# An odd mixer's running sums spread by DMA instead of by matmul, its heads worked in pairs, and each pair's products queued later

## The chip, the cores and the metric

The kernel runs on one core of a Trainium2 chip. The metric is the device time of one execution in microseconds, as the median of several runs. The engines are PE (TensorE, the matmuls), ACT (ScalarE), DVE (VectorE), POOL (GpSimd) and SP (SyncE, which issues most DMAs). Each takes its own queue of instructions in order and waits for others by semaphores.

## What is computed

One inference step of a two-layer decoder trunk: 256 prompt tokens and 8 sequences of 4 sampled tokens (288 columns in all), model width 2048, f32 data. Layer 0 mixes tokens by a gated MLP and sparse attention, layer 1 (the odd one) by a Mamba-2 scan, and each layer ends in a gated feed-forward block. The change touches the scan of layer 1 alone: 64 heads in 8 groups, 128-token chunks for the prompt, 4-token chunks for the samples.

```python
def segsum(a):
    t = a.shape[-1]
    cs = jnp.cumsum(a, axis=-1)
    d = cs[..., :, None] - cs[..., None, :]
    return jnp.where(jnp.tril(jnp.ones((t, t), bool)), d, NEG)

def ssd(x, dt, a, bm, cm, h0):
...
    da = (dt * a).reshape(b, c, q, g, e).transpose(0, 3, 4, 1, 2)
    acs = jnp.cumsum(da, axis=-1)
    cb = jnp.einsum('bcign,bcjgn->bgcij', cc, bc)
    mix = cb[:, :, None] * jnp.exp(segsum(da))
    y_diag = jnp.einsum('bgecij,bcjgep->bcigep', mix, xdt)
...
    y_off = jnp.einsum('bcign,bcgepn->bcigep', cc, st[:, :-1]) * jnp.exp(acs).transpose(0, 3, 4, 1, 2)[..., None]
```

For each head the running sums `acs` have to stand along the free axis in every partition (index i), so that those of index j, one to a partition, can be taken from them.

## The kernel before

The projections set the pace. Every weight matrix is streamed from HBM in loads of 512 KB (`load_w`, line 636; five buffers `wraw`, 8 blocks of 128x128 each), and `convert` (line 644) cuts each half of a load, called a piece here, into a high part `whi` (ACT) and a low part `wlo` (DVE), four pieces ahead of PE. A block then costs three products of 128x288 (high by high, high by low, low by high), so a piece is 12 matmuls.

The program is written out by a planner when it is built. `Clock` holds a model of the engines' times, each instruction is an `Op`, and jobs (generators) hand their instructions to `step` (line 561). A job may yield an instruction, a number (it sleeps for so many planned us), a list of tiles (it sleeps until the planner believes them ready), or a wish for a buffer. An instruction goes into its engine's queue at the point of the main loop at which the planner believes that it can start; for PE, 0.4 us (`HOP` and `MARGIN`) are added behind another engine. A DMA is planned with 2.0 us and its bytes at 360 GB/s (lines 395 and 397). Jobs made with `back` take turns, three at a time, and leave at most 2.5 us of work planned ahead on an engine. The real engines wait by semaphores, so a wrong plan costs waits, not errors.

Phase m1 is the odd mixer. Its projection yields, for each of 8 groups, B, C, four x blocks (`xbc`, through a convolution) and four gates (`z`). With the fourth gate of a group the scan's job `ssd(g)` (line 1213) starts; the fourth gate's evacuation first waits for the norm of the group before (`evac_z`, line 1195, `finish_ssd`). `ssd` transposes x and B, forms the masked products `cbm`, the end state `st`, and starts in the background `ssd_old` (the old states' part, into `xdd`), four `ssd_heads` (one for each pair of heads, line 1324) and `ssd_norm` (line 1379). `ssd_new` updates and stores eight states meanwhile: a product `xst` by `bst` into PSUM, a scaling of `h0` on POOL, an addition on DVE (h<-h,ps), a store by SP.

In `ssd_heads` each head is worked by itself: PE multiplies a column of a selector matrix (`selc`, 128 rows) by the running sums, held as high and low halves in `csh`, which gives the sums in all 128 partitions of a PSUM bank (`pl`); ACT takes Relu of three parts with each partition's own sum as bias into `L`, an exponential of the second chunk into `ec`, and two exponentials of `L`; POOL multiplies `ec` by C; DVE multiplies `L` by `cbm` into `mx` (prompt) and `mxs` (samples). There are two buffers of `L`, four each of `mx`, `ec` and `mxs`. After the second head a `Burst` of 20 products of the pair (`mx`, `ec`, `srep`, `mxs`) goes into PE's queue, and its result passes through DVE and POOL into y and the sum of squares. All PSUM tiles named `ps` come from five banks. All instructions have the planner's line, L391, in the profile; so tiles' names tell them apart.

Of the kernel before, what the change touches and what calls it, by code (L numbers as in the profile page):

```python
# [18 lines left out]
PT, ST, T = 256, 32, 288  # L19
# [103 lines left out]


MATS = {}
for _n, _w in (("tle", 128), ("tgt", 128), ("ble", 32), ("bgt", 32), ("selc", 64), ("srep", 32), ("srepT", 128),
               ("tmask", 256)):
    MATS[_n] = (sum(w for _, w in MATS.values()), _w)
NMAT = sum(w for _, w in MATS.values())
# [2 lines left out]
def const_mats():  # L132

    i = np.arange(128)
    t = np.arange(ST)
    same = t[:, None] // NS == t // NS
    m = dict(
        tle=i[:, None] <= i, tgt=i[:, None] > i,
        ble=same & (t[:, None] <= t), bgt=same & (t[:, None] > t),
        selc=i[:, None] % 64 == np.arange(64),  # L140
        srep=i[:, None] % 32 == t, srepT=t[:, None] == i % 32,
        tmask=np.broadcast_to(np.arange(NB)[:, None] == t // NS, (128, NB, ST)).reshape(128, -1),
    )
    out = np.zeros((128, NMAT), np.float32)
    for k, v in m.items():
        out[:v.shape[0], MATS[k][0]:MATS[k][0] + v.shape[1]] = v
    return out
# [374 lines left out]
class Trunk:  # L522
# [137 lines left out]
    def run(self):  # L660
        tc, nc = self.tc, self.nc
        with ExitStack() as st:
            pool = lambda n, b, **k: Slots(st.enter_context(tc.tile_pool(name=n, bufs=b, **k)), b, self.clk)
            self.cst = pool("cst", 1)
            self.wraw = pool("wraw", 5)
            self.wsp = pool("wsp", AHEAD + 1)
            self.xp = pool("xp", 1)
            self.rms = pool("rms", 4)
            self.hsp = pool("hsp", 1, space=bass.MemoryType.DRAM).tile([128, KD, T], F32, name="hsp")
            self.pmain = pool("pmain", PMAIN, space=bass.MemoryType.PSUM)  # L670
            self.pold = pool("pold", 1, space=bass.MemoryType.PSUM)
            self.pside = pool("pside", 7 - PMAIN, space=bass.MemoryType.PSUM)
            st.enter_context(tc.manual_schedule())
            self.body()
# [343 lines left out]
    def enter_m1(self, l):  # L1018
        nc = self.nc
        self.job(self.make_rstd())  # L1020
        self.nbg = 3
        one = self.pool("one", 1)
        self.wk = self.pool("wk", 2)
        self.w3 = self.pool("w3", 3)
        self.w4 = self.pool("w4", 4)
        self.w8 = self.pool("w8", NB)
        self.zr = self.pool("zr", 12)
        t = lambda name, shape, dt=F32: one.tile(shape, dt, name=name)
        self.cmat = t("cmat", [128, NMAT])
        nc.sync.dma_start(self.cmat, self.I["cmat"])  # L1030
        self.y2 = t("y2", [128, 16, T])
        self.cx = deque(t(f"cx{i}", [128, 315]) for i in range(3))
        for c in self.cx:
            nc.gpsimd.memset(c[:, 0:3], 0.0)
        self.sw = t("sw", [128, 48, 5])
        self.selc = t("selc", [128, 64], F32R)
        self.dtt = t("dtt", [128, 3, 64])
        self.dat = t("dat", [128, 3, 64])
        self.cs = t("cs", [128, 3, 64])
        self.dec = t("dec", [128, 3, 64])  # L1040
        self.ecr = t("ecr", [128, 64])
        self.et1 = t("et1", [128, 64])
        self.ets = t("ets", [128, NB, 64])
        self.csh = t("csh", [128, T], F32R)
        self.xdt = t("xdt", [128, 2, 512])
        self.xdd = t("xdd", [128, 2, 512])

        self.xds = t("xds", [128, 512])
        nc.gpsimd.memset(self.xds[64:128], 0.0)
        self.mxs = deque(t(f"mxs{i}", [128, ST]) for i in range(4))  # L1050
        for z in self.mxs:
            nc.gpsimd.memset(z, 0.0)
        self.xst = t("xst", [96, 512], F32R)
# [12 lines left out]
        self.job(self.odd_consts())  # L1066
        self.job(self.load_h(), 20.0)

    def odd_consts(self):
        nc = self.off  # L1070
        yield nc.vector.tensor_scalar(self.sw[:, :, 0:4], self.P("sw", 0, 192).rearrange("p (c k) -> p c k", k=4), 0.5, None,
                                      op0=OP.mult)
        yield nc.vector.tensor_scalar(self.sw[:, :, 4], self.P("sb", 0, 48), 0.5, None, op0=OP.mult)
        yield nc.vector.tensor_copy(self.selc, self.M("selc"))
        self.flags.add("consts")

    def load_scv(self, g):
# [15 lines left out]
    def dt_chain(self, z):  # L1093
        nc, wk = self.off, self.w3
        e = yield wk.want([64, T], F32, name="dz")
        q = yield wk.want([64, T], F32, name="dz")
# [18 lines left out]
        ps = yield self.pside.want([128, 2, 3, 64], F32, name="ps")  # L1115
# [22 lines left out]
        yield self.mm(p2[:, 0:128], da[:, 0], self.M("tle"), start=True, stop=True)  # L1138
        yield self.mm(p2[:, 128:256], da[:, 1], self.M("tle"), start=True, stop=True)
        yield self.mm(p2[:, 256:288], das, self.M("ble", 32), start=True, stop=True)  # L1140
        yield nc.scalar.copy(self.csh[:64], p2)
        yield nc.vector.tensor_tensor(self.csh[64:128], p2, self.csh[:64].bitcast(F32), op=OP.subtract)
        self.rel(p2)
        p3 = yield self.pside.want([128, 512], F32, name="ps")
        yield self.mm(p3, self.ones[:32].to_broadcast([32, 128]), dam.rearrange("p b h -> p (b h)"), start=True, stop=True)
        yield nc.scalar.activation(self.ets.rearrange("p b h -> p (b h)"), p3, AF.Exp)
# [177 lines left out]
    def ssd_heads(self, g, q):  # L1324

        nc, wk = self.off, self.wk
        C = self.C[g]
        mx, ce, ms = [], [], []
        for e in range(2):
            h = 8 * g + 2 * q + e  # L1330
            m = yield self.w4.want([128, PT], F32, name="mx")
            ec = yield self.w4.want([128, 128], F32, name="ec")
            L = yield wk.want([128, T], F32, name="L")
            pl = yield self.pside.want([128, T], F32, name="ps")
            yield self.mm(pl, self.selc[:, h:h + 1].to_broadcast([128, 128]), self.csh, start=True, stop=True)
            for lo, hi, r, c in ((0, 128, 128, 0), (128, 256, 128, 1), (256, 288, 32, 2)):
                yield nc.scalar.activation(L[:r, lo:hi], pl[:r, lo:hi], AF.Relu, bias=self.cs[:r, c, h:h + 1], scale=-1.0)
            yield nc.scalar.activation(ec, pl[:, 128:256], AF.Exp)
            self.rel(pl)
            yield nc.scalar.activation(L[:, :PT], L[:, :PT], AF.Exp, scale=-1.0)  # L1340
            yield nc.scalar.activation(L[:32, PT:], L[:32, PT:], AF.Exp, scale=-1.0)
            yield nc.gpsimd.tensor_tensor(ec, ec, C[:, 128:256], op=OP.mult)
            yield nc.vector.tensor_tensor(m[:, :PT], L[:, :PT], self.cbm[:, :PT], op=OP.mult)
            while not self.mxs:
                yield 0.3
            z = self.mxs.popleft()
            yield nc.vector.tensor_tensor(z[:32], L[:32, PT:], self.cbm[:32, PT:], op=OP.mult)
            ms.append(z)
            self.rel(L)
            mx.append(m)  # L1350
            ce.append(ec)
        while "old" not in self.sdone:
            yield 0.4
        py = yield self.pside.want([128, T], F32, name="ps")

        oh = [(e, py[64 * e:64 * e + 64], slice(128 * q + 64 * e, 128 * q + 64 * e + 64)) for e in range(2)]
        ops = [self.mm(o[:, 0:128], self.xdt[:, 0, hc], mx[e][:, 0:128], start=True, stop=True) for e, o, hc in oh]
        ops += [self.mm(o[:, 128:256], self.xdt[:, 1, hc], mx[e][:, 128:256], start=True, stop=False) for e, o, hc in oh]
        ops += [self.mm(o[:, 128:256], self.st[:, hc], ce[e], start=False, stop=True) for e, o, hc in oh]
        ops += [self.mm(o[:, 256:288], self.xdd[:, 0, hc], self.M("srep"), start=True, stop=False) for e, o, hc in oh]  # L1360
        ops += [self.mm(o[:, 256:288], self.xds[:, hc], ms[e], start=False, stop=True) for e, o, hc in oh]
        yield Burst(ops)
        self.mxs.extend(ms)
        k = 4 * g + q
        y = self.yraw(k)
        yield nc.vector.scalar_tensor_tensor(y, y, self.P("sd", k), py, op0=OP.mult, op1=OP.add)
# [904 lines left out]
```

## Time and profile before

| | us |
|---|---|
| median of 3 runs | 3082.39 |
| lowest and highest run | 3081.61, 3086.01 |
| profiled execution, its time | 3080.35 |
| profiled execution, its span | 3078.6 |

The profile is of one execution. Busy time of an engine is the time in which it worked on an instruction. PE's rows give a matmul's own duration; they overlap in the pipeline, so a busy PE may take a new product every 133 ns while each lasts 295. PEld, the weight load, is a row of its own. "Idle before" is the time an engine stood still just ahead of an instruction, and the name behind it is what ended the wait.

### The profile page before, as it was taken

What the parts mean: (1) busy time and instruction counts of PE and PEld (TensorE: products, weight loads), DVE (VectorE), ACT (ScalarE), POOL (GpSimd) and SP (SyncE); (2) the same over time, 40 slices, a digit from 0 to 9 for tenths busy, and PEclk for the clock granted to TensorE, in tenths of its full rate; (3) what the DMA queues carried; (4) which work ended last, traced back from release to release, by engine and by line L of the source; (5) the groups of instructions that cost most, each with busy time, mean ns of one, the idle gap of its engine ahead of it and who ended that gap; (6) DMA issues with size and microseconds to landing.
All of it is one profiled execution on the core that took longest, in us unless ns stands there. A gap on an engine that the chain in (4) does not pass through costs nothing.

```text
span 3078.6 us, 62211 instructions
## 1 busy us (share of the span) xinstructions
PE 3043.6 (99%) x23073; PEld 2943.9 (96%) x23073; DVE 2166.0 (70%) x4593; ACT 1614.4 (52%) x3229; POOL 724.6 (24%) x1029
## 2 busy tenths in 40 slices
PE   9999999999999999999999999999999999999999
PEld 8887889999999999999999999999999999999999
DVE  7876567775577557668888888885777647755764
ACT  6766545554455445555555555554455435544553
POOL 4535433100000000123445555530310000000000
PEclk8999999999999999999999999999999999999999
DMA  8987885444444444564555555554454444444454
GB/s 316 348 282 249 277 282 176 165 165 165 164 165 165 165 166 164 184 222 142 188 198 191 191 191 185 196 179 174 161 172 166 166 166 164 165 165 165 165 177 146
DMA packets 189760, 587.41 MB, mean 191 GB/s; under 512 B 23280, under 2 KB 43280, under 8 KB 189456
## 3 DMA queue, kind: packets, MB, share of 16 engines
q1 hardware_dynamic: 170256, 516.31, 48.7%
q0 software_dynamic: 19200, 67.12, 6.3%
q8 instruction: 182, 2.98, 0.4%
q14 instruction: 122, 1.00, 0.1%
HBM read 555.57 MB, written 27.78 MB: 189 GB/s over the span
## 4 chain that ended last, share of the span: by engine, by line
PE 89%; DVE 4%; POOL 3%; issue 1%; DMA 1%; ACT 1%; SPq 0%; DVEq 0%; ACTq 0%; POOLq 0%
PE acc L391 79%; PE ps L391 9%; DVE wlo L391 1%; PE po L391 1%; POOL ec L391 1%; DVE h L391 1%; DMA st<-in_ccmp,ptc 1%; POOL ssq L391 1%; POOL nrm L391 1%; DVE cv L391 1%; ACT whi L391 0%; DMA st<-in_cselv,ptv 0%; DVE mxs L391 0%; POOL st L391 0%; ACT L L391 0%
## 5 line engine op out<-in xcount | busy, mean ns | idle before, releaser
L391 DVE TENSOR_TENSOR wlo<-wraw,whi 128x512 fp32r<-128x512 f32 x1720 | 1230.4, 718 | 809.3 <-ACT whi L391 793.5
L391 ACT CAST whi<-wraw 128x512 fp32r<-128x512 f32 x1720 | 1058.5, 619 | 1187.6 <-PE acc L391 1062.0
L391 PE MATMUL acc<-xh,whi 128*128 128x288 f32 x5158 | 1552.9, 301 | 3.8 <-DVE h L391 3.4
L391 PE MATMUL acc<-xl,whi 128*128 128x288 f32 x5158 | 1524.4, 296 | 0.5 <-DVE xl L391 0.5
L391 PE MATMUL acc<-xh,wlo 128*128 128x288 f32 x5158 | 1519.8, 295 | 0.2 <-DVE wlo L391 0.2
L391 PEld LDWEIGHTS acc<-xh,whi 128*128 128x128 f32 x5158 | 969.7, 188 | 23.8 <-issue 15.1
L391 PEld LDWEIGHTS acc<-xl,whi 128*128 128x128 f32 x5158 | 971.4, 188 | 6.0 <-issue 3.8
L391 PEld LDWEIGHTS acc<-xh,wlo 128*128 128x128 f32 x5158 | 973.5, 189 | 0.7 <-DVE wlo L391 0.7
L391 PE MATMUL acc<-hidh,whi 128*128 128x288 f32 x1380 | 407.9, 296 | 0.0
L391 PE MATMUL acc<-hidl,whi 128*128 128x288 f32 x1380 | 407.1, 295 | 0.0
L391 PE MATMUL acc<-hidh,wlo 128*128 128x288 f32 x1380 | 406.1, 294 | 0.0
L391 POOL COPY fcv<-hx 128x18 f32<-128x18 f32 x176 | 37.3, 212 | 1399.4 <-DVE hx L391 1399.4
L391 PEld LDWEIGHTS acc<-hidh,wlo 128*128 128x128 f32 x1380 | 259.8, 188 | 0.0
L391 PEld LDWEIGHTS acc<-hidl,whi 128*128 128x128 f32 x1380 | 259.0, 188 | 0.0
L391 PEld LDWEIGHTS acc<-hidh,whi 128*128 128x128 f32 x1380 | 258.6, 187 | 0.0
L391 DVE SCALAR_TENSOR_TENSOR cv<-hx,prm,cv 128x304 f32<-128x304 f32 x352 | 185.9, 529 | 0.0
L391 POOL DMA_INDIRECT st<-in_ccmp,ptc x64 | 92.0, 1438 | 108.6 <-DVE S L391 22.3
L391 ACT ACTIVATE cv<-hx,prm 128x304 f32<-128x304 f32 x176 | 112.5, 641 | 0.8
L391 PE MATMUL ps<-xh,whi 128*128 128x288 f32 x314 | 94.6, 301 | 0.0
L391 PE MATMUL ps<-xh,wlo 128*128 128x288 f32 x314 | 93.1, 296 | 0.7 <-DVE wlo L391 0.7
L391 PE MATMUL ps<-xl,whi 128*128 128x288 f32 x314 | 93.1, 297 | 0.6 <-DVE xl L391 0.6
L391 DVE SCALAR_TENSOR_TENSOR cv<-cx,sw,cv 128x312 f32<-128x312 f32 x144 | 91.7, 641 | 2.6 <-ACT cv L391 2.6
(356 smaller groups left out, 2800.2 us busy)
## 6 DMA issues: line engine op xcount, KB each, us to landing
wraw<-in_w SPq DMA_DIRECT2D x859, 512.0 KB
h<-in_h SPq DMA_DIRECT2D x64, 256.0 KB
out_h<-h SPq DMA_DIRECT2D x64, 256.0 KB
st<-in_cselk SPq DMA_DIRECT2D x64, 128.0 KB
st<-in_cwk POOLq DMA_DIRECT2D x8, 512.0 KB
st<-in_cwv POOLq DMA_DIRECT2D x8, 512.0 KB
h<-in_xT SPq DMA_DIRECT2D x18, 144.0 KB
hsp<-h SPq DMA_DIRECT2D x4, 576.0 KB
```

What stands on the lines that cost most here:

```text
L391: self.f(*self.args, **self.kw)
```

## The change

The running sums, which a DMA now writes once to a buffer `csd` in HBM (64 rows of 288 columns), are read back for each pair of heads, two rows at a time, into all partitions of `L`, by a DMA on SP whose source is repeated. The selector matrix, `csh` and the products that used them are gone. The pair is worked together: `L`, `mx`, `ce` and `ms` hold both heads, and the two exponentials of `L`, the one into `ce` and the products on POOL and DVE take both heads in one instruction; the Relus stay one for each head and part. `L`, `mx`, `ce` and `ms` have two buffers each, of twice the size. ACT's work is planned 1.2 us after the planned landing, and the burst 2.5 us after the planned end of its operands.

```diff
...
+            self.csd = pool("csd", 1, space=bass.MemoryType.DRAM).tile([64, T], F32, name="csd")
...
-        self.w4 = self.pool("w4", 4)
...
-        self.selc = t("selc", [128, 64], F32R)
...
-        self.csh = t("csh", [128, T], F32R)
...
-        self.mxs = deque(t(f"mxs{i}", [128, ST]) for i in range(4))
+        self.mxs = deque(t(f"mxs{i}", [128, 2, ST]) for i in range(2))
...
-        yield nc.vector.tensor_copy(self.selc, self.M("selc"))
+        pass
...
-        yield nc.scalar.copy(self.csh[:64], p2)
-        yield nc.vector.tensor_tensor(self.csh[64:128], p2, self.csh[:64].bitcast(F32), op=OP.subtract)
+        csh = yield wk.want([64, T], F32, name="dz")
+        yield nc.scalar.copy(csh, p2)
         self.rel(p2)
+        yield nc.sync.dma_start(self.csd, csh)
...
-        mx, ce, ms = [], [], []
+        h0 = 8 * g + 2 * q
+
+        L = yield wk.want([128, 2, T], F32, name="L")
+        yield nc.sync.dma_start(L, self.csd[None, h0:h0 + 2, :].to_broadcast([128, 2, T]))
+        mx = yield wk.want([128, 2, PT], F32, name="mx")
+        ce = yield wk.want([128, 2, 128], F32, name="ec")
+        yield [L]
+        yield 1.2
+        yield nc.scalar.activation(ce, L[:, :, 128:256], AF.Exp)
         for e in range(2):
-            h = 8 * g + 2 * q + e
-            m = yield self.w4.want([128, PT], F32, name="mx")
-            ec = yield self.w4.want([128, 128], F32, name="ec")
-            L = yield wk.want([128, T], F32, name="L")
-            pl = yield self.pside.want([128, T], F32, name="ps")
-            yield self.mm(pl, self.selc[:, h:h + 1].to_broadcast([128, 128]), self.csh, start=True, stop=True)
             for lo, hi, r, c in ((0, 128, 128, 0), (128, 256, 128, 1), (256, 288, 32, 2)):
-                yield nc.scalar.activation(L[:r, lo:hi], pl[:r, lo:hi], AF.Relu, bias=self.cs[:r, c, h:h + 1], scale=-1.0)
-            yield nc.scalar.activation(ec, pl[:, 128:256], AF.Exp)
-            self.rel(pl)
-            yield nc.scalar.activation(L[:, :PT], L[:, :PT], AF.Exp, scale=-1.0)
-            yield nc.scalar.activation(L[:32, PT:], L[:32, PT:], AF.Exp, scale=-1.0)
-            yield nc.gpsimd.tensor_tensor(ec, ec, C[:, 128:256], op=OP.mult)
-            yield nc.vector.tensor_tensor(m[:, :PT], L[:, :PT], self.cbm[:, :PT], op=OP.mult)
...
-            yield nc.vector.tensor_tensor(z[:32], L[:32, PT:], self.cbm[:32, PT:], op=OP.mult)
...
+                yield nc.scalar.activation(L[:r, e, lo:hi], L[:r, e, lo:hi], AF.Relu, bias=self.cs[:r, c, h0 + e:h0 + e + 1],
+                                           scale=-1.0)
+        yield nc.scalar.activation(L[:, :, :PT], L[:, :, :PT], AF.Exp, scale=-1.0)
+        yield nc.scalar.activation(L[:32, :, PT:], L[:32, :, PT:], AF.Exp, scale=-1.0)
+        yield nc.gpsimd.tensor_tensor(ce, ce, C[:, None, 128:256].to_broadcast([128, 2, 128]), op=OP.mult)
+        yield nc.vector.tensor_tensor(mx, L[:, :, :PT], self.cbm[:, None, :PT].to_broadcast([128, 2, PT]), op=OP.mult)
+        while not self.mxs:
+            yield 0.3
+        ms = self.mxs.popleft()
+        yield nc.vector.tensor_tensor(ms[:32], L[:32, :, PT:], self.cbm[:32, None, PT:].to_broadcast([32, 2, ST]), op=OP.mult)
+        self.rel(L)
...
+        yield [mx, ms, ce]
+        yield 2.5
         yield Burst(ops)
-        self.mxs.extend(ms)
+        self.mxs.append(ms)
```

The 20 products of the burst are the same, with the operands' new names.

## Rows read from the trace of the kernel before

**Rows 1.** The page: the span, the engines' busy times.
```profile
span 3078.6 us, 62211 instructions
...
PE 3043.6 (99%) x23073; PEld 2943.9 (96%) x23073; DVE 2166.0 (70%) x4593; ACT 1614.4 (52%) x3229; POOL 724.6 (24%) x1029
```

**Rows 2.** Windows: length, busy PE, PEld, DVE, ACT, POOL (instructions), clock, DMA share, GB/s.
```profile
1440.00:2062.00 622.00, 610.11 (x4806) 571.54 (x4805) 542.80 (x1080) 357.39 (x887) 318.67 (x345) 1.00 0.55 187
...
2070.00:2150.00 80.00, 80.00 (x602) 79.95 (x602) 47.04 (x91) 34.76 (x62) 0.00 (x0) 1.00 0.51 177
```

**Rows 3.** PE's groups by form in 1440:2062: count, busy, mean ns, idle before, releasers.
```profile
L391 PE MATMUL ps<-xst,bst 96*128 96x512 f32 x64 | 23.1, 406 | 3.5 <-DVE h L391 3.5
...
L391 PE MATMUL ps<-csh,selc 128*128 128x288 f32 x64 | 19.2, 320 | 2.4 <-DVE xdd L391 1.9 <-DVE h L391 0.5
...
L391 PE MATMUL ps<-ec,st 128*64 128x128 f32 x128 | 15.6, 275 | 0.9 <-POOL ec L391 0.4
...
L391 PE MATMUL ps<-mxs,xds 128*64 128x32 f32 x128 | 13.0, 224 | 5.1 <-DVE mxs L391 5.1
```

**Rows 4.** PE's timeline in the second group: start, duration, instruction, idle before.
```profile
1535.92 0.39 PE L391 MATMUL ps<-xst,bst 96*128 96x512 f32 x1
1536.14 0.29 PE L391 MATMUL ps<-csh,selc 128*128 128x288 f32 x1
...
1537.06 0.39 PE L391 MATMUL ps<-xst,bst 96*128 96x512 f32 x1
1537.77 0.40 PE L391 MATMUL ps<-csh,selc 128*128 128x288 f32 x1 [0.31 <-DVE xdd L391]
```

**Rows 5.** SP's timeline, then DMA share and GB/s in 2016:2020, forty slices.
```profile
2016.18 0.33 SPq L391 DMA_DIRECT2D dz<-hsp  x1
...
DMA  0000000003063986986992409579999959969897
GB/s 0 0 0 0 0 0 0 0 0 82 0 81 104 161 184 230 300 288 133 146 216 41 82 41 328 205 287 410 369 369 410 410 246 532 451 246 533 328 410 328
```

**Rows 6.** Waits in 1440:2062: ACT's for L, then SP's: total, times, longest.
```profile
ACT L L391 <- DVE mxs L391: 25.1, 15, 2.2
...
SPq L391 <- DVE h L391: 85.5, 49, 7.7
SPq L391 <- DMA out_h<-h: 45.3, 44, 3.6
```

**Rows 7.** Windows of wlo alone from the start: PE's products, DVE's conversions so far.
```profile
0.00:1520.60 1520.60, 973.50 (x3299) 624.01 (x3300) 586.09 (x829) 0.99 0.60 209
...
0.00:1543.90 1543.90, 984.12 (x3336) 630.85 (x3336) 593.30 (x836) 0.99 0.60 207
```

**Rows 8.** ACT's groups by form in 1440:2062.
```profile
L391 ACT CAST whi<-wraw 128x512 fp32r<-128x512 f32 x305 | 183.3, 615 | 130.0 <-PE acc L391 116.2 <-issue 7.6 <-DMA h<-in_h 2.0
...
L391 ACT ACTIVATE L<-L 128x256 f32<-128x256 f32 x64 | 25.6, 401 | 0.0
...
L391 ACT ACTIVATE ec<-ps 128x128 f32<-128x128 f32 x64 | 16.1, 251 | 0.0
```

**Rows 9.** DVE's groups by form in 1440:2062.
```profile
L391 DVE TENSOR_TENSOR h<-h,ps 128x512 f32<-128x512 f32 x64 | 41.3, 673 | 0.0
L391 DVE TENSOR_TENSOR mx<-L,cbm 128x256 f32<-128x256 f32 x64 | 33.5, 524 | 0.0
L391 DVE TENSOR_TENSOR mxs<-L,cbm 32x32 f32<-32x32 f32 x64 | 28.3, 443 | 0.0
```

**Rows 10.** POOL's group of ec in 1440:2062.
```profile
L391 POOL TENSOR_TENSOR ec<-ec,zt 128x128 f32<-128x128 f32 x64 | 56.1, 887 | 14.6 <-ACT ec L391 13.7
```

**Rows 11.** The tile mxs: duration in ns, shortest, median and longest.
```profile
L391 DVE TENSOR_TENSOR mxs<-L,cbm x64: 171/173/1022, 1459.0 to 2059.7; 32x32 f32<-32x32 f32 x64
```

**Rows 12.** DVE's timeline at a group's end: last norm product, fourth gate.
```profile
1598.75 0.50 DVE L391 SCALAR_TENSOR_TENSOR h<-h,prm,ps 128x288 f32<-128x288 f32 x1
...
1601.71 0.45 DVE L391 SCALAR_TENSOR_TENSOR zt<-acc,rstd 128x288 f32<-128x288 f32 x1
```

More of the change, by code (lines that the diff above doesn't have):

```diff
@@ L125 @@
 MATS = {}
-for _n, _w in (("tle", 128), ("tgt", 128), ("ble", 32), ("bgt", 32), ("selc", 64), ("srep", 32), ("srepT", 128),
+for _n, _w in (("tle", 128), ("tgt", 128), ("ble", 32), ("bgt", 32), ("srep", 32), ("srepT", 128),
                ("tmask", 256)):
@@ L139, in const_mats @@
         ble=same & (t[:, None] <= t), bgt=same & (t[:, None] > t),
-        selc=i[:, None] % 64 == np.arange(64),
         srep=i[:, None] % 32 == t, srepT=t[:, None] == i % 32,
@@ L1327, in ssd_heads @@
         C = self.C[g]
-        mx, ce, ms = [], [], []
-        for e in range(2):
-            h = 8 * g + 2 * q + e
-            m = yield self.w4.want([128, PT], F32, name="mx")
-            ec = yield self.w4.want([128, 128], F32, name="ec")
-            L = yield wk.want([128, T], F32, name="L")
-            pl = yield self.pside.want([128, T], F32, name="ps")
-            yield self.mm(pl, self.selc[:, h:h + 1].to_broadcast([128, 128]), self.csh, start=True, stop=True)
-            for lo, hi, r, c in ((0, 128, 128, 0), (128, 256, 128, 1), (256, 288, 32, 2)):
-                yield nc.scalar.activation(L[:r, lo:hi], pl[:r, lo:hi], AF.Relu, bias=self.cs[:r, c, h:h + 1], scale=-1.0)
-            yield nc.scalar.activation(ec, pl[:, 128:256], AF.Exp)
-            self.rel(pl)
-            yield nc.scalar.activation(L[:, :PT], L[:, :PT], AF.Exp, scale=-1.0)
-            yield nc.scalar.activation(L[:32, PT:], L[:32, PT:], AF.Exp, scale=-1.0)
-            yield nc.gpsimd.tensor_tensor(ec, ec, C[:, 128:256], op=OP.mult)
-            yield nc.vector.tensor_tensor(m[:, :PT], L[:, :PT], self.cbm[:, :PT], op=OP.mult)
-            while not self.mxs:
-                yield 0.3
-            z = self.mxs.popleft()
-            yield nc.vector.tensor_tensor(z[:32], L[:32, PT:], self.cbm[:32, PT:], op=OP.mult)
[L1348 to L1351, printed above, removed]
@@ L1356, in ssd_heads @@
         oh = [(e, py[64 * e:64 * e + 64], slice(128 * q + 64 * e, 128 * q + 64 * e + 64)) for e in range(2)]
-        ops = [self.mm(o[:, 0:128], self.xdt[:, 0, hc], mx[e][:, 0:128], start=True, stop=True) for e, o, hc in oh]
-        ops += [self.mm(o[:, 128:256], self.xdt[:, 1, hc], mx[e][:, 128:256], start=True, stop=False) for e, o, hc in oh]
-        ops += [self.mm(o[:, 128:256], self.st[:, hc], ce[e], start=False, stop=True) for e, o, hc in oh]
+        ops = [self.mm(o[:, 0:128], self.xdt[:, 0, hc], mx[:, e, 0:128], start=True, stop=True) for e, o, hc in oh]
+        ops += [self.mm(o[:, 128:256], self.xdt[:, 1, hc], mx[:, e, 128:256], start=True, stop=False) for e, o, hc in oh]
+        ops += [self.mm(o[:, 128:256], self.st[:, hc], ce[:, e], start=False, stop=True) for e, o, hc in oh]
         ops += [self.mm(o[:, 256:288], self.xdd[:, 0, hc], self.M("srep"), start=True, stop=False) for e, o, hc in oh]
-        ops += [self.mm(o[:, 256:288], self.xds[:, hc], ms[e], start=False, stop=True) for e, o, hc in oh]
+        ops += [self.mm(o[:, 256:288], self.xds[:, hc], ms[:, e], start=False, stop=True) for e, o, hc in oh]
+        yield [mx, ms, ce]
+        yield 2.5
         yield Burst(ops)
-        self.mxs.extend(ms)
+        self.mxs.append(ms)
         k = 4 * g + q
```

## The prediction

> **What bounds the kernel now.** First the page: PE is busy 3043.6 of 3078.6 us (99%), DVE 70%, ACT 52%, POOL 24% [rows 1]. PE takes its queue in order, so only two things can move the end: a matmul taken off PE, or a gap in its queue closed or opened. Next the windows, because the shares of the page are averages [rows 2]. In 1440:2062, the stretch of the odd mixer in which the groups' heads are worked, PE is busy 610.1 of 622.0 us, DVE 542.8 (87%), ACT 357.4, POOL 318.7, the DMA engines 0.55, at full granted clock. In 2070:2150, where only projections run, 602 matmuls fill 80.00 us without a break: 132.9 ns for one 128x288 product, the price of a place in PE's queue. The changed code runs in the first stretch alone, and PE's gaps there are 622.0 - 610.1 = 11.9 us.
>
> Third, PE's groups by form say where these 11.9 us lie [rows 3]: 5.1 before the products of mxs, 3.5 before xst (the state update), 2.4 before the selector products (csh, selc), 0.9 before ec. All but the last wait for DVE. Fourth, the timeline shows what a gap really costs [rows 4]: a selector product behind an xst starts 0.22 us after it where nothing holds it (1535.92 to 1536.14) and 0.71 us after it where 0.31 us is printed as idle. That is 0.49 lost: the printed gap and 0.18 us for the pipeline to fill again. I add 0.18 for each gap below.
>
> **The change part by part.** *Selector products removed.* 64 products of 128x288, the form of the price above: 64 x 0.1329 = 8.5 us off PE. Nothing hides them, and their PSUM banks fall free as well.
>
> *Transfers added.* 32 loads, one for a pair: 2 x 288 x 4 = 2304 B into each of 128 partitions, 288 KB. All of them are 9.4 MB in 622 us, 15 GB/s beside 187 GB/s at a share of 0.55 [rows 2], so the share rises to about 0.60: no time by bandwidth. For the landing, the nearest row is the reload of 144 KB from the same kind of buffer [rows 5]: issued at 2016.18, the DMA engines start on it 0.7 us later (slices of 0.1 us), and with the weight load behind it they move up to 0.37 MB in each us. From below, 288 KB land 0.7 + 0.8 = 1.5 us after issue; from above, with one 512 KB load in front (1.4 us) and at the 0.16 MB in a us of the burst's first ten slices (1.9 us), 4.0 us. I take 3.0, near the middle, since SP's queue usually holds one weight load. The planner counts 2.0 us and 0.82 for the bytes (lines 395 and 397), and the change adds 1.2, so ACT's work is put into its queue as if the rows came 4.0 us after issue: covered, by 1.0 us.
>
> By the Trainium skill, "DMA: Bandwidth & Descriptors" (Anatomy of one DMA; Latency and other measured facts), a DMA costs about 2.0 us and its bytes at 436 GB/s, an estimate of 2.7 us here, and an HBM access 0.2 us on average but 2 us at high load, which would make some 4.5. No row shows that load latency; by it ACT would wait 0.5 us at a pair, and the sum would not move, as ACT's lead below covers it.
>
> *SP's queue.* A load of L waits in SP for the last DVE reader of its buffer. Before, it was ACT that waited for that: 25.1 us in 15 waits, at most 2.2 [rows 6]. Behind it on SP stand weight loads, the stores of the states and the next states' loads; SP already waits 85.5 us for DVE h, 45.3 for stores to land, and 7.7 us at most in one wait [rows 6]. Who waits for that in the end is the weight conversion. Its lead over PE: 829 pieces converted against 3299 / 4 = 824.8 used at 1520.6, 4.2 pieces of 12 matmuls (1.6 us each), but only 836 against 834.0 at 1543.9, the tightest point of a group: 2 pieces or 3.2 us [rows 7]. I put 2 us of new PE gaps on this, between 0 and 8.
>
> *ACT, DVE and POOL.* Per pair ACT has 9 instructions for 12: the Relus keep their number, and the 64 + 64 exponentials of 128x256 and 128x128 (401 and 251 ns) become 32 + 32 of twice the width; with 150 ns for each 128 columns that is 25.6 + 16.1 against 22.4 + 12.8 us [rows 8]. DVE: 64 mx at 524 ns and 64 mxs at 443 become 32 of 128x512 (673 ns by h<-h,ps) and 32 small ones: 61.8 us become some 36 [rows 9]. POOL: 64 ec of 887 ns become 32 of once to twice that: 56.1 us become 28 to 57 [rows 10]. None is PE's, so I price this at nothing: ACT still sits idle 116.2 us waiting for PE to free conversion buffers [rows 8]. But DVE, which PE's gaps wait for, gains some 25 of 543 us.
>
> The mxs rows have one shape and yet run from 171 to 1022 ns [rows 11]: up to 0.85 us that the planner does not know of. That is what opens the gap in the middle of the burst. The Trainium skill, "SBUF — State Buffer" (Who interferes with whom), has a rule for it: a DVE instruction with two SBUF inputs is blocked, for the whole of the other's instruction, by a GpSimd one that reads SBUF. The rows agree as far as they go, POOL's ec alone lasting 0.89 us on the mean. By that rule half as many DVE instructions can be caught, but a joined one of 128x512 shuts POOL out for longer; the sum would be the same by both, unless POOL's work became late, which is the third rival.
>
> *The delay of the burst.* Now a pair's products go into PE's queue when the planner thinks the operands done (plus its 0.4 us), and a DVE instruction 0.85 us late stands in PE's way. With 2.5 us more it is over before PE comes there. That takes away the mxs gaps, 5.1 + 7 x 0.18 = 6.4 us, and those of ec, 0.9 + 2 x 0.18 = 1.3. If DVE were late by over 2.9 us they would be back at 0.9 us for a group. Nothing stands behind the wait on PE, since the burst is simply queued later. Behind the burst come y, POOL's squares, the norm, and the next group's start.
>
> *The other gaps.* The selector products waited for a PSUM bank that DVE had still to read (2.4 + 8 x 0.18 = 3.8 us). DVE stays as late, but two banks less are in use: I take half, 1.9, as gone and half as passed on to the next taker, between 0 and 3.8. The xst gaps (3.5 + 7 x 0.18 = 4.8) are of the same kind; I leave them, between 0 and 4.8 gained.
>
> Sum, against the profiled execution: 8.5 + 6.4 + 1.3 + 1.9 - 2 = 16.1 us off 3080.35, which is 3064.2. Its time lies 2.04 us under the median of the runs shown (3082.39), so I forecast 3066 us. The best case of these bounds is 24.8 off (3058), the worst 8.5 + 7.7 - 8 = 8.2 off (3074).
>
> **The rivals.** *The gaps come back (3076).* DVE is busy 87% of the stretch, and PE's gaps wait for it; the next reader of a bank, or a later burst, may wait as the selector products did. Then only the 8.5 us of matmuls are gained and up to 4 are lost again: 3074 to 3080. For it: three of four groups of gaps name DVE. Against it: DVE loses 25 us of work and two banks become free.
>
> *L comes late and starves PE (3091, the slower side).* SP is in order; one wait of 7.7 us in front of a load of L makes the load late, ACT, in order too, stands before the Relus, and the conversions behind them miss their time. It decides where L is later than planned by more than the lead of 3.2 us. For 4.8 us of lateness in the two later pairs of each group (the first two find free buffers), 16 x (4.8 - 3.2) = 26 us of PE gaps against 16.1 + 2 gained: 3091. For it: the waits of SP above. Against it: those waits are mostly before the work is due, and the planner places a load where it believes the buffer free. The skill's 2 us at high load would take part of that lead, not all.
>
> *The group's chain grows (3083).* A burst queued later, by 2.5 us, and POOL work put off, push the norm; the fourth gate's evacuation waits for it, and PE soon waits for the evacuation. The last multiplication of the norm ends at 1599.25, that evacuation starts at 1601.71: 2.5 us of room in each group [rows 12]. If the heads took 5 us longer, 7 x 2.5 = 17.5 us would come back, and nothing be left. Against it: a group's heads went through two L buffers in four rounds of one head each, and now go in two rounds of two, so the stage should shrink, delay included.
>
> **How the numbers follow.** Forecast 0.70 (3058 to 3074), gaps come back 0.14, late L 0.10, longer chain 0.06. A measurement of this kernel can tell about 0.2% (6 us) from no change, so faster means under 3076.2: 0.70 and under half of the 0.14, 0.76; within: 0.08 and 0.04, 0.12; slower: 0.10 and the bad end of the last, 0.12. The range of 8 in 10 goes from just under the best case to where most of the first rival lies: 3057 to 3079.
>
> **What will show it.** Right: in the stretch, PE's groups hold no selector product, the gaps before mxs and ec are near zero, those before xst at most 3.5 us, and the stretch is about 16 us shorter than 622. ACT's wait for L names its DMA and stays under 1 us a pair. Wrong: gaps before the projections' products that name whi or wlo (late L), gaps before xst or bank users grown to 8 us (gaps come back), or a gap behind the fourth gate of a group (chain). What is outside the stretch should not move at all.

## The result and the profile after

The changed kernel takes 3111.1 us (median of 4 runs, 3107.94 to 3114.92) against 3082.0 for the kernel before beside it: ratio 1.0092, interval 1.0080 to 1.0104. The forecast was 3066. The profiled execution took 3107.94 us with a span of 3106.1, 27.5 over that of before [rows 1].

The page and the window of the odd mixer (columns as in [rows 2]):

```profile
span 3106.1 us, 61890 instructions
...
PE 3041.6 (98%) x23009; PEld 2944.1 (95%) x23009; DVE 2193.2 (71%) x4527; ACT 1612.5 (52%) x3133; POOL 709.9 (23%) x995
```
```profile
1440.00:2062.00 622.00, 583.67 (x4507) 548.79 (x4506) 544.72 (x980) 338.20 (x746) 286.55 (x296) 0.98 0.56 192
```

PE's idle time in these 622 us is 38.3 us where it was 11.9, and the mean granted clock is 0.98 where it was 1.00. Behind the scan nothing moved: 940 us from 2110 on hold 938.66 us of busy PE in both kernels. PE's groups by form in 1440:2062 show where the idle time went (count, busy, mean ns, idle before):

```profile
L390 PE MATMUL ps<-xst,bst 96*128 96x512 f32 x58 | 21.7, 394 | 0.0
L390 PE MATMUL ps<-mx,xdt 128*64 128x128 f32 x224 | 18.4, 285 | 21.1 <-DVE mx L390 21.1
L390 PE MATMUL ps<-ec,st 128*64 128x128 f32 x112 | 10.9, 273 | 0.0
L390 PE MATMUL ps<-mxs,xds 128*64 128x32 f32 x112 | 8.2, 225 | 0.1
L390 PE MATMUL ps<-ones,ssq 128*96 128x1 f32 x42 | 5.1, 237 | 17.1 <-POOL ssq L390 17.1
```

All gaps of before [rows 3] are gone: mxs, xst, ec and the selector products. Two new ones stand in their place, each at the head of something that PE takes in order: the burst, which now waits for mx, and the norm's sums, which wait for the sum of squares that POOL makes last in a group.

The sums of the third group can be followed through three engines. In the kernel after (PE, DVE, POOL timelines: start, duration, instruction, idle before):

```profile
1668.36 0.29 PE L390 MATMUL ps<-mxs,xds 128*64 128x32 f32 x4
...
1676.00 0.67 PE L390 MATMUL ps<-ones,ssq 128*96 128x1 f32 x6 [2.36 <-POOL ssq L390]
```
```profile
1671.08 1.12 DVE L390 SCALAR_TENSOR_TENSOR cv<-cx,sw,cv 128x312 f32<-128x312 f32 x2
1672.11 0.51 DVE L390 SCALAR_TENSOR_TENSOR h<-h,prm,ps 128x288 f32<-128x288 f32 x1
```
```profile
1672.70 1.18 POOL L390 TENSOR_TENSOR h<-h,zt 128x288 f32<-128x288 f32 x1 [2.10 <-DVE h L390]
1673.96 0.79 POOL L390 TENSOR_TENSOR nrm<-h 128x288 f32<-128x288 f32 x1
1674.83 1.12 POOL L390 TENSOR_TENSOR ssq<-ssq,nrm 128x288 f32<-128x288 f32 x1
```

The last burst ends at 1668.65, but DVE, busy without a break, takes its result (h<-h,prm,ps) only at 1672.11, 3.5 us later. In the kernel before, the second group's last burst ends at 1576.77 and DVE is there at 1577.18:

```profile
1577.18 0.50 DVE L391 SCALAR_TENSOR_TENSOR h<-h,prm,ps 128x288 f32<-128x288 f32 x1
1579.51 1.13 POOL L391 TENSOR_TENSOR ssq<-ssq,nrm 128x288 f32<-128x288 f32 x1
1580.79 0.59 PE L391 MATMUL ps<-ones,ssq 128*96 128x1 f32 x6
```

So DVE comes 3 us later behind the burst than it did (3.5 to 3.7 us in each of the first seven groups, 0.4 before); POOL's three instructions follow in 3.3 us; PE, sent to the sums by the plan, stands still for 2.36 us. The kernel before had next to no room at this place: in seven of its eight groups POOL's last sum of squares ended 0.15 us ahead of PE's sums, as in the last two lines.

What comes behind such a gap is the second half of the loss. Windows of the kernel after, around it:

```profile
1672.00:1675.90 3.90, 1.64 (x13) 1.41 (x11) 3.90 (x6) 0.97 (x2) 3.04 (x3) 1.00 0.32 117
1676.00:1677.50 1.50, 1.50 (x13) 1.50 (x14) 1.36 (x5) 0.11 (x1) 0.00 (x0) 1.00 0.78 243
1677.60:1680.90 3.30, 3.30 (x16) 3.30 (x16) 1.01 (x3) 2.76 (x5) 0.00 (x0) 0.50 0.18 62
1681.00:1684.30 3.30, 3.30 (x27) 3.30 (x26) 1.61 (x5) 1.24 (x2) 0.00 (x0) 1.00 0.56 171
```

After PE has begun again, 3.4 us are granted at 0.50, that is 1.2 in place of 2.4 GHz, although PE is busy in all of them: 16 products where the window behind takes 27. In all the kernel after has 23.9 us at 0.50 in the scan; the kernel before has none. In the stretch shown a product starts 0.24 us after the one ahead of it, 0.13 us in the window behind: 45% of the time is lost, so that the 23.9 us cost about 11. The Trainium skill, "TensorE: Matmul & The Clock Gate" (Terms), prices the time at the lower rate by the share of pulses left out, half of it here. The trace comes near that, with 45%.

### The profile page after: what moved, and what is told of

It is laid out like the page before. It is cut to its first block, busy times and chain, and to the rows that moved or that the text cites. A ratio compares the mean times of both kernels' runs of the same rounds, so it can differ in the third digit from the quotient of the medians.

```text
span 3106.1 us, 61890 instructions
## 1 busy us (share of the span) xinstructions
PE 3041.6 (98%) x23009; PEld 2944.1 (95%) x23009; DVE 2193.2 (71%) x4527; ACT 1612.5 (52%) x3133; POOL 709.9 (23%) x995
## 4 chain that ended last, share of the span: by engine, by line
PE 88%; DVE 4%; DMA 4%; issue 2%; ACT 2%; POOL 1%; SPq 0%; DVEq 0%; ACTq 0%; POOLq 0%
PE acc L390 78%; PE ps L390 9%; DMA st<-in_ccmp,ptc 1%; PE po L390 1%; DVE cv L390 1%; DVE wlo L390 1%; DMA st<-in_cselv,ptv 1%; DMA out_h<-h 1%; ACT whi L390 1%; DVE mx L390 1%; DMA h<-in_h 1%; DVE h L390 0%; POOL ssq L390 0%; POOL nrm L390 0%; DVE mxs L390 0%
## 5 line engine op out<-in xcount | busy, mean ns | idle before, releaser
L390 DVE SCALAR_TENSOR_TENSOR cv<-cx,sw,cv 128x312 f32<-128x312 f32 x144 | 101.3, 703 | 0.2
```

The lines of the kernel that those rows point to most:

```text
L390: self.f(*self.args, **self.kw)
```

## The experiments

Each kernel was run beside the kernel before, and its ratio is against those runs. To compare the kernels, each profile was reduced to four terms against before: 8.5 us less where the selector products are gone; PE's waits between 1440 and 2110 less the 11.3 us in 24 waits of before; 0.18 us for each wait more; half of the time at 0.50. Beside the sum stands what the trace shows from the scan's first transposition (1440.1 in before) to the end, less 1638.5 us, which is before's.

| kernel | median us | ratio (95%) | PE's waits us (count) | at 0.50 us | sum | shown |
|---|---|---|---|---|---|---|
| the change | 3111.1 | 1.0092 (1.0080 to 1.0104) | 38.6 (29) | 23.9 | +31.7 | +26.3 |
| before_delay | 3109.6 | 1.0097 (1.0078 to 1.0116) | 29.3 (23) | 30.7 | +33.2 | +28.5 |
| after_no_delay | 3116.1 | 1.0111 (1.0094 to 1.0128) | 36.9 (18) | 51.2 | +41.6 | +34.8 |
| after_delay7 | 3094.9 | 1.0048 (1.0031 to 1.0064) | 27.2 (29) | 17.1 | +16.9 | +15.1 |
| pairs_by_pe | 3117.4 | 1.0121 (1.0104 to 1.0138) | 34.9 (14) | 30.7 | +37.2 | +34.1 |
| after_split_mx | 3121.9 | 1.0130 (1.0114 to 1.0147) | 39.2 (34) | 34.1 | +38.3 | +39.2 |
| after_pad | 3108.2 | 1.0090 (1.0072 to 1.0107) | 32.6 (19) | 34.1 | +29.0 | +25.3 |
| after_sum_delay | 3085.6 | 1.0018 (1.0006 to 1.0030) | 22.9 (20) | 6.8 | +5.8 | +2.2 |
| after_pad_sum | 3082.7 | 1.0002 (0.9992 to 1.0011) | 18.4 (28) | 6.8 | +2.7 | +1.1 |
| after_norm | 3085.2 | 1.0004 (0.9995 to 1.0014) | 18.3 (28) | 6.8 | +2.6 | -0.4 |
| before_norm | 3105.2 | 1.0064 (1.0048 to 1.0081) | 27.0 (28) | 20.5 | +26.7 | +23.3 |
| before_delay_norm | 3108.2 | 1.0075 (1.0059 to 1.0092) | 27.4 (21) | 27.3 | +29.2 | +23.8 |
| pairs_by_pe_norm | 3092.8 | 1.0033 (1.0022 to 1.0045) | 20.1 (23) | 6.8 | +12.0 | +10.1 |
| after_room | 3097.7 | 1.0044 (1.0027 to 1.0061) | 29.0 (30) | 13.7 | +17.1 | +15.8 |
| pad_sum_free | 3078.8 | 0.9986 (0.9976 to 0.9996) | 14.8 (20) | 6.8 | -2.3 | -4.1 |
| before_delay_free | 3088.1 | 1.0018 (1.0009 to 1.0028) | 16.9 (13) | 10.2 | +8.7 | +6.3 |
| no_delay_sum | 3112.0 | 1.0097 (1.0078 to 1.0116) | 34.7 (15) | 47.8 | +37.1 | +29.4 |
| delay7_sum_free | 3074.1 | 0.9974 (0.9964 to 0.9984) | 12.1 (16) | 3.4 | -7.4 | -8.1 |
| before_free | 3083.3 | 1.0003 (0.9994 to 1.0011) | 11.3 (24) | 0 | 0 | 0.0 |

The terms give most of the size and, roughly, the order; they run ahead of the trace by up to 8 us where much time is at 0.50 (`after_split_mx`, 0.9 us short, is the exception). Little of that time falls on waits of PE, where it would cost nothing: 0.6 of 23.9 us in the change, 1.9 of 47.8 in `no_delay_sum`. That 45% of it is lost in the stretch shown, and not half, would take 1.2 us off the change's sum; the rest of the difference is not explained.

### Which part of the change does it: one part alone, one part undone

`before_delay` is the kernel before with the burst's delay alone:

```diff
+        yield [*mx, *ms, *ce]
+        yield 2.5
         yield Burst(ops)
```

> The kernel before with only the delay added: a pair's burst is queued 2.5 us after the planned end of its operands; transfers and joined instructions are left out. Theory 'late plan' (what hurts in the changed kernel is that L and the joined products come later than planned, the delay itself is sound): the gaps before the products of mxs and ec go (about 6 to 9 us of PE), the rest stays, 3074 to 3077 us. Rival 'the delay' (a burst queued later pushes the squares and the norm, and the norm's sums then hold PE): gaps of 2 to 2.5 us before the sums in each group as in the changed kernel, 3092 to 3100 us.

The delay alone costs what the whole change does, more than either theory allowed (3092 to 3100 by 'the delay'), and not where that one had it. mxs no longer waits, but:

```profile
PE ps L391 <- DVE hl L391: 11.7, 6, 6.2
PE ps L391 <- DVE rb L391: 6.0, 7, 0.9
PE ps L391 <- POOL ssq L391: 4.4, 2, 2.7
```

hl and rb are the last steps of the norm: PE transposes the scale (hl) and spreads it (rb).

`after_no_delay` leaves the two delay lines of the change out:

> The changed kernel without the delay of the burst. 'Late plan': each burst then waits up to 2.5 us more for mx, four in a group, the waits let the other engines catch up, so the wait before the norm's sums shrinks; 3112 to 3140 us. Rival 'the delay': without it the norm's sums wait no more, 16 to 20 us come back, about 3092 us.

It is no better, as 'late plan' said. The waits for mx grow to 35.1 us in 15, longest 3.5, those for ssq shrink to 1.8, and 51.2 us are at 0.50.

`after_delay7` has `yield 7.0` for `yield 2.5` there:

> The changed kernel with a delay of 7.0 us in place of 2.5. 'Late plan': mx is late by 3.6 to 4.0 us against its planned end, so all gaps before the bursts close (about 4 us a group, 31 us in all); the wait before the norm's sums stays at 2.5 us or the fourth gate now waits in the plan, which takes back up to 4.5 us a group; 3085 to 3105 us. Rival 'the delay': the norm moves by 4.5 us more, the gaps before its sums or behind the fourth gate grow by as much, 3125 us or more.

That is within the range of 'late plan'. No wait for mx is left, but 8.9 us for ssq, 7.0 for hl, 5.3 for rb.

`pairs_by_pe` works in pairs with the delay, but spreads by PE as before (to make room, the convolution's weights stay in the buffer that they were loaded to):

```diff
...
-        yield nc.sync.dma_start(L, self.csd[None, h0:h0 + 2, :].to_broadcast([128, 2, T]))
...
+            yield self.mm(pl, self.selc[:, h:h + 1].to_broadcast([128, 128]), self.csh, start=True, stop=True)
...
```

> The changed kernel with the running sums spread by PE again (64 selector products into PSUM, ACT's Relus and the exponential into ec read PSUM, one head at a time), while L, mx, ec and mxs stay joined in pairs and the burst stays delayed by 2.5 us. To make room in SBUF the halved convolution weights stand in their parameter tile. If the transfer's landing (5.3 us where 2.8 and 1.2 are planned) is the cause, the gaps before the bursts fall to a few tenths: 3085 us or less although 8.5 us of matmuls are back. If the joined instructions are the cause (mx of 128x512 takes 1.3 us where 0.6 is planned), the gaps stay near 1.1 to 1.5 us for a burst: 3110 to 3120 us.

```profile
PE ps L391 <- POOL ssq L391: 26.3, 7, 3.8
PE ps L391 <- DVE xdd L391: 8.6, 7, 1.3
```
```profile
L391 DVE TENSOR_TENSOR mx<-L,cbm x32: 671/679/1228, 1468.2 to 2093.4; 128x512 f32<-128x512 f32 x32
```

Without the transfers no burst waits for mx, and the joined mx is short (median 679 ns; 1299 in the change). So the waits for mx hang on the transfer, not on the joining alone. But the sums wait all the more (they do not hang on the transfer), and the time of 3085 us or less, expected for that case, did not come.

`after_split_mx` keeps all but the joined mx:

```diff
-        yield nc.vector.tensor_tensor(mx, L[:, :, :PT], self.cbm[:, None, :PT].to_broadcast([128, 2, PT]), op=OP.mult)
+        for e in range(2):
+            yield nc.vector.tensor_tensor(mx[:, e], L[:, e, :PT], self.cbm[:, :PT], op=OP.mult)
```

> The changed kernel, but mx is worked head by head (two DVE instructions of 128x256 in place of one of 128x512). Theory 'caught': the joined mx is late because a long two-input DVE instruction is blocked by a POOL one (1299 ns mean against 0.6 planned); then two short ones are together nearer to plan, the 21.5 us of PE's waits for DVE mx fall below 10, and the time is about 3095 us. Theory 'late chain': the rows of L land 1.3 us behind their due time and DVE works without a break behind them, so the length of one instruction matters little: waits for mx stay at 17 to 26 us, time 3105 to 3117.

At 3122 it is slower than either theory had it; the 17.6 us for mx are in the range of 'late chain', and ssq takes 21.6. Shorter DVE instructions do not mend it; but two halves of 884 ns each at the median are together longer than the joined 1299, so this does not show that the length of mx is without effect.

### Is it the plan's due times?

`after_pad` puts 3.7 for 1.2 behind L's planned landing; `after_sum_delay` queues the sums later; `after_pad_sum` does both:

```diff
+        yield [self.ssq]
+        yield 3.0
         yield from self.sums(ps, self.ssq)
```

> The changed kernel with 3.7 us in place of 1.2 between the planned landing of L and the work on it: the plan now has L 2.5 us later, behind its real landing. Theory 'wrong due time': only the plan of L is off; with it mended the waits for mx (21.5 us) go below 5, norm sums stay at about 17, time 3080 to 3090. Theory 'late chain': DVE and POOL work the heads no sooner, and the wait moves on to the norm: waits for mx fall to 5 to 10, those for ssq rise to 20 or more, time 3100 to 3112.

> The changed kernel, and PE's norm sums (ones, ssq) are queued 3.0 us after the plan believes the last squares done. Theory 'wrong due time': the 2.4 us gap before the sums of each group (17.1 us in all) and the stretch at the lower granted clock behind it (1.7 us) go, 29 us in all, and the waits for mx stay: time about 3082. Theory 'late chain': the norm's next steps (hl, rb) or the fourth gate are then what PE waits for, and no more than 10 us come back: 3100 to 3111.

> Both of the two edits before it: 3.7 us behind the landing of L, and 3.0 us behind the squares. Theory 'wrong due time': all of PE's waits of the heads (21.5 + 17.1 us) and the low clock behind them are gone, and what remains is the kernel before less its 64 selector products and mxs gaps: 3065 to 3075. Theory 'late chain': the group is as long as its chain of DVE and POOL work, the waits stand before hl, rb or the fourth gate's products, and the time is 3095 to 3110.

`after_pad` did what 'late chain' said: mx fell to 2.6 us, ssq rose to 19.7, hl came up with 4.5, the time stayed. But the 3.0 us ahead of the sums gave back 25 of the 29 us, as 'wrong due time' said:

```profile
PE ps L390 <- DVE mx L390: 11.9, 14, 1.3
PE acc L390 <- DVE cx L390: 5.3, 3, 2.3
PE ps L390 <- DVE hl L390: 4.5, 1, 4.5
PE ps L390 <- DVE rb L390: 0.8, 1, 0.8
PE ps L390 <- POOL ssq L390: 0.4, 1, 0.4
```

All but 0.4 of ssq's 17.1 us are gone, 17.1 of the 23.9 us at 0.50 too, and eight of the 22 waits for mx. Both edits together gave 3083, between the ranges of the two theories (3065 to 3075, 3095 to 3110). Of the 18.4 us of waits left, 9.1 are for hl and rb, most of them at one place. PE's timeline of the seventh group of `after_pad_sum`:

```profile
2003.51 0.29 PE L390 MATMUL acc<-xh,wlo 128*128 128x288 f32 x1
2008.68 0.32 PE L390 MATMUL ps<-ident,hl 96*6 96x96 f32 x1 [4.88 <-DVE hl L390]
2009.82 0.61 PE L390 MATMUL ps<-rb,ones_r 128*128 128x288 f32 x1 [0.82 <-DVE rb L390]
2010.23 0.44 PE L390 MATMUL acc<-xh,whi 128*128 128x288 f32 x1
```

Between hl and rb there is no projection: PE was given nothing else to do.

### Delays of the norm, and the plan's own wait

The next four kernels put the whole norm off: 3.0 us ahead of the sums, 0.5 ahead of hl (5.5 in the last group), 1.5 ahead of rb; `after_norm` has the 3.7 behind L too.

```diff
...
         yield nc.vector.tensor_tensor(hl[:, k:2 * k], r, hl[:, :k].bitcast(F32), op=OP.subtract)
+        if late:
+            yield [hl]
+            yield late
...
```

> The changed kernel with 3.7 us behind the landing of L, 3.0 us ahead of the norm sums, 0.5 us (5.5 in the last group) ahead of the transposition of hl and 1.5 us ahead of the spread of rb: every product of the heads and the norm is queued behind its operands' real end. Theory 'wrong due time': the 4.9 us of hl, the 4.2 us of rb and the low clock behind the former go, some 13 us under the kernel with the first two delays alone (3083): 3068 to 3072, which is faster than before. Theory 'late chain': the group is as long as DVE's and POOL's work makes it, another wait of 1 to 2 us a group takes their place (the fourth gate's evacuation, cx or zt), and the time is 3080 to 3090.

> The kernel before with the delays of the norm alone (3.0 us ahead of the sums, 0.5 and in the last group 5.5 ahead of hl, 1.5 ahead of rb), nothing else changed. The kernel before shows no wait for ssq, hl or rb, so theory 'wrong due time' gives no gain here: 3079 to 3086. Theory 'late chain', by which the room at the end of a group is 2.5 us and the norm is put off by 5: 7 x 2.5 = 17.5 us lost, 3095 to 3105. A gain of over 6 us would mean that the delays of the norm help by themselves, whatever the change does.

> The kernel before with the change's delay of the burst (2.5 us behind its operands) and the delays of the norm. The burst's delay alone made it 3110, with waits for hl (11.7 us), rb (6.0) and ssq (4.4) and 31 us at half clock. Theory 'wrong due time': these go, and the mxs gaps stay away: 3073 to 3080. Theory 'late chain': a burst 2.5 us later makes the group longer wherever its end is queued: 3100 to 3110.

> The kernel with the heads in pairs and the burst delayed, but the running sums spread by PE's selector products, and the delays of the norm. Without these it was 3117, with 26.3 us of waits for ssq in 7 waits. Theory 'wrong due time': 26.3 + 7 x 0.18 us of gaps and some 12 us of low clock go: 3074 to 3082, and by comparison with the kernel that loads L instead (same delays) the transfers are worth the 8.5 us of selector products. Theory 'late chain': 3105 to 3115.

`after_norm` gained nothing: hl 5.1, rb 4.9. A delay does not mend these two waits. And `before_norm`, which only puts the norm of the old kernel off, lost 21 us, as 'late chain' said (`before_delay_norm` too, at 3108, with 11.1 us for hl, 8.5 for xdd and 6.4 for rb):

```profile
PE ps L391 <- DVE hl L391: 8.0, 3, 6.2
PE ps L391 <- DVE h L391: 5.5, 7, 2.0
PE ps L391 <- DVE rb L391: 4.3, 5, 0.9
```

So there is a second mechanism: `evac_z` (line 1195) has the plan wait for the last group's norm ahead of the fourth gate's evacuation. If the norm is not through by then, the planner gives PE only the norm's own steps, and PE waits for each in turn. `pairs_by_pe_norm` came down by 25 us but stayed 7.6 over `after_norm`, which loads L instead: close to the 8.5 us of the selector products, with nearly the same waits (20.1 and 18.3 us) and time at 0.50 (6.8 us each).

Taking that wait away tells the two apart:

```diff
-        if u.i == 3 and u.g:
-            self.finish_ssd(u.g - 1)
```

`pad_sum_free` and `before_delay_free` are `after_pad_sum` and `before_delay` with it; `after_room` keeps the wait and shortens the chain (2.4 us behind L; 2.5 ahead of the sums, 0.2 in the seventh group); `no_delay_sum` is `after_sum_delay` without the burst's delay.

> The changed kernel with 2.4 us behind the landing of L (1.2 in the change) and 2.5 us ahead of the norm sums, 0.2 in the seventh group, whose norm met the fourth gate's evacuation 4.9 us late when its sums were put off by 3.0. Theory 'deadline': the waits for hl (4.9) and rb (4.2) nearly vanish, the waits for mx stay at 3 to 7 us and the seventh group's ssq at 2.4: 3073 to 3079. Theory 'chain work': the waits reappear elsewhere at the same size, 3082 to 3087.

> The changed kernel with 3.7 us behind L and 3.0 us ahead of the sums (3083 in that form), and without the plan's wait for the last group's norm ahead of the fourth gate's evacuation (line 1196). Theory 'deadline': hl's 4.9 us, rb's 4.2 us, 7 refills of 0.18 and 3.4 us of low clock go, and the selector products' 8.5 us show at last: about 3069. Theory 'chain work': the norm is late anyway, the next group's transpositions start later, and the time stays at 3080 to 3086.

> The kernel before with the burst's delay alone (3110 in that form, waits for hl 11.7, rb 6.0, ssq 4.4 us and 31 us at half clock), and without the plan's wait for the norm (line 1196 of the changed kernel). Theory 'deadline': the waits for hl and rb go with their low clock, those for ssq (4.4) stay: 3078 to 3086. Theory 'chain work': the groups push each other on, 3100 to 3112.

> The changed kernel without the delay of the burst, and with 3.0 us ahead of the norm sums. Without either it was 3116, with 35.1 us of waits for mx and 1.8 for ssq. Both theories: the sums were hardly waited for there, so the waits for mx and their low clock stay, 3110 to 3118; against 3086 with the delay and the same sums this prices the delay at some 30 us. If it fell to 3090 or lower, the delay would be worth nothing once the sums are mended.

`before_delay_free` fell from 3110 to 3088, 2 us above the range of 'deadline': the waits for hl and rb (17.7 us) are gone, and 20.5 of the 30.7 us at 0.50. So most of what the delay cost the old kernel is this wait. `pad_sum_free` got 3.9 us, not 13: hl and rb no longer wait, but mx does again (8.8 us in 8). `after_room` came out slower than both theories: ssq 9.9, cx 8.6, rb 6.0; with less delay the sums were waited for again, while rb still met the wait. `no_delay_sum` stayed at 3112 (mx 34.7): with the sums mended the burst's delay is worth some 25 us.

Last, `delay7_sum_free` has 7.0 for the burst, 3.0 for the sums and no wait in `evac_z`; `before_free` is the kernel before without that wait.

> The changed kernel with the burst 7.0 us behind its operands in place of 2.5, 3.0 us ahead of the norm sums, and without the plan's wait for the norm (line 1196). With 7.0 alone (3095) there was no wait for mx, but 8.9 us for ssq, 7.0 for hl and 5.3 for rb. Theory 'deadline and due times': all of these are covered now, what remains is below 6 us of waits and no low clock, and the selector products' 8.5 us show: 3066 to 3073. Theory 'chain work': some other wait of 1 to 2 us a group comes up (xst, cx, the next group's state), 3077 to 3086.

> The kernel before without the plan's wait for the norm ahead of the fourth gate's evacuation, nothing else. Its trace shows no wait for ssq, hl or rb, so theory 'deadline' has nothing to gain here: 3079 to 3087. A gain of over 6 us would mean that part of what the changed kernel got back by the same edit is not the change's.

The window of the scan, `before` first, then `delay7_sum_free`, and the longest waits of the latter:

```profile
1440.00:2110.00 670.00, 658.11 (x5168) 619.50 (x5167) 569.06 (x1130) 376.77 (x918) 321.27 (x348) 1.00 0.55 187
1440.00:2110.00 670.00, 657.61 (x5143) 621.38 (x5142) 569.58 (x1057) 373.65 (x814) 291.17 (x308) 1.00 0.61 203
```
```profile
PE acc L390 <- DVE wlo L390: 3.9, 5, 1.5
PE acc L390 <- DVE cx L390: 3.6, 5, 1.6
PE ps L390 <- POOL bst L390: 1.9, 2, 1.3
```

That is 3074.1 us, 0.9974 of before (0.9964 to 0.9984), the fastest kernel here, though a little above the 3066 to 3073 expected: 12.1 us of waits were left in 16 where below 6 had been foreseen, and 3.4 us at 0.50. The waits are nearly before's 11.3, and the 8.5 us of selector products show. `before_free` is at 1.0003: the edit is worth nothing to the old kernel.

## Why the prediction was wrong, step by step

*Selector products, 8.5 us: right as far as can be seen.* No run takes them out alone, but `pairs_by_pe_norm` against `after_norm` gives 7.6 us, and `delay7_sum_free`, with nearly before's waits, 8.1.

*Gaps of mxs, ec, bank and xst: gone, but partly by luck.* All fell to 0.1 us or less, xst's too, which were left standing in the sum. For mxs the reason given holds: in `before_delay` the delay alone removes them. But in the change 22 of the 32 bursts wait at their head, for mx, so that part of the waiting may only have moved there; in `before_delay`, where they do not, waits for ec (1.8 us), for banks (xdd, 2.1) and for xst (h, 2.8) are still there.

*L lands after 3.0 us: too low.* The tile L of the kernel after:

```profile
L390 SPq DMA_DIRECT2D L<-csd x32: 327/426/927, 1452.0 to 2078.1; - x32
L390 DVE TENSOR_TENSOR mx<-L,cbm x32: 672/1299/1530, 1467.0 to 2088.3; 128x512 f32<-128x512 f32 x32
...
DMA to landing us min/median/max: 4.4/5.3/5.8
```

The landing takes 4.4 to 5.8 us, beyond the upper bound of 4.0 worked out from the reload, and 1.3 us at the median behind the plan of 4.0. The Trainium skill, "DMA: Bandwidth & Descriptors" (Anatomy of one DMA; Latency and other measured facts), gave an estimate of 2.7 us, by its price of a DMA that GpSimd issues (SP issues this one), and of 4.5 with an HBM access at high load. Both are under the measured median. ACT waited 13.0 us in 9 waits for it, 0.4 us a pair on the mean and so under 1 as foreseen, and no conversion was late for PE (no wait for whi or wlo): the rival of a starved PE did not come. But the lateness went on to mx.

*"With 2.5 us more it is over before PE comes there": failed at mx.* The step put DVE's lateness at 0.85 us, the spread of mxs. With L 1.3 us late and mx at 1.3 us in place of 0.67 by the shortest row, the burst waited 22 times, 21.5 us, up to 1.2 us at a time. These two make 1.9 us, which the 2.5 us and the plan's 0.4 would have covered; waits of 1.2 us behind that cover mean that mx was some 4 us late, and where the other 2 come from is not shown. The sentence on the bound (late by over 2.9 us) had the mechanism; its size was a third of what came. The rule of the Trainium skill, "SBUF — State Buffer" (Who interferes with whom), that the prediction used for mxs fits mx as well. The trace agrees as far as it goes: the one mx of 672 ns is the only one with no POOL instruction beside it, and the other 31 have a median of 1.30 us. In `pairs_by_pe`, though, 23 of 32 have one beside them too, at a median of 0.69 us, so this does not explain the long mx by itself; and `after_split_mx` shows that splitting them buys nothing.

*"Nothing stands behind the wait on PE": the step that cost most.* Behind the burst stand y, POOL's squares and the sums, and the sums are PE's own. They were looked at for the room at the group's end alone, and there the forecast holds: the last norm product and the fourth gate are as far apart as before [rows 12],

```profile
1609.60 0.51 DVE L390 SCALAR_TENSOR_TENSOR h<-h,prm,ps 128x288 f32<-128x288 f32 x1
...
1612.56 0.45 DVE L390 SCALAR_TENSOR_TENSOR zt<-acc,rstd 128x288 f32<-128x288 f32 x1
```

and no wait for hl or rb is in the trace. What was not asked is where PE meets the sums. The room there was 0.15 us, not 2.5; the change waits 17.1 us there, and `after_sum_delay` gives these back with 25 us in all. The delay and the pairs do it together: `after_no_delay` waits 1.8 us for ssq, `before_delay`, without pairs, 4.4.

*DVE gains 25 us, "I price this at nothing".* mx and mxs took 35.2 and 11.7 us in 1440:2062 where 61.8 stood [rows 9], about 8 us less for the same number of heads and not 25; the convolution's cv took 91.7 us in 126 instructions, at 728 ns against 657 before. DVE was no freer.

*A gap costs its length and 0.18 us: failed.* It was read from a gap of 0.31 us [rows 4]. A gap of 2.36 us brought 3.4 us at 0.50 with it, 1.5 us more. The forecast had no term for that, and it is some 11 of the 29 us.

*The rivals.* "The gaps come back" had the place (a later burst waits for DVE), but bounded the loss by the old gaps, 4 us; the change opened 38.6 us of waits where there had been 11.3. "The group's chain grows" did not decide this kernel, but its mechanism is real: `before_delay_free` won 22 of the 29 us of `before_delay` back, and the waits for hl and rb are nearly half of those in `before_norm` (12.3 of 27.0 us). The room of 2.5 us a group was read rightly; the price of crossing it was too small, since PE then waits for each step of the norm and loses clock behind it.

What stays open: why DVE comes to the last burst of a group 3 us and more later than before, even without transfers (4.9 us behind it in `pairs_by_pe`), and what makes L land late. Neither was tried by itself.

## What to carry to other kernels

Where a planner orders an in-order engine, a change of delays must be followed to every later instruction of the same job on that engine, not only to the one that it protects; here 3 us ahead of the norm's sums were worth 25 us. Before products are queued later, look for points at which the plan itself waits for the end of that chain. Price a gap on PE by the granted clock behind it as well: here gaps of up to 0.7 us brought no stretch at the lower clock, and one of 2.4 us cost some 1.7 times its length.

## What the runs showed of the hardware

Gaps of up to 0.72 us, 24 of them in the kernel before, left the granted clock at 1.00 (2.4 GHz); with the change, the gaps of 2.4 to 2.6 us ahead of the sums went with 3.4 us at 0.50 (1.2 GHz) in six groups of seven, in one of them with twice that. In the group shown this began 1.6 us after PE had started again (1676.00 to 1677.6) and fell on full work; in the first group it began 0.6 us before. Size alone does not decide it: a gap of 1.60 us was followed by such a stretch in `delay7_sum_free`, while gaps of 1.70 us in `pad_sum_free` and of 3.34 us in `after_no_delay` were not. A read of 288 KB from a DRAM buffer, each row repeated into 128 partitions, landed 4.4 to 5.8 us after its issue beside a weight stream of some 190 GB/s, while the 512 KB weight loads of the same queue took 3.3 at the median.
